# First down projection of a hybrid decoder layer with weights as the wide operand and results by rows

## The chip, the cores and the metric

The kernel runs on one core of one Trainium2 chip. The metric is the device time of one execution in microseconds (us), lower is better. The core's engines appear below as PE (TensorE, matrix products; PEld is its loading of the stationary operand), DVE (VectorE), ACT (ScalarE), POOL (GpSimd) and SP (SyncE, which here only issues DMAs). Each engine works through its own queue in order, and waits on semaphores for what other engines and transfers produce.

## The reference

One layer over 512 tokens of 1024 features in fp32: two feed-forward blocks around a mixer, each added to the running x.

```python
x = x + 0.5 * swiglu(rmsnorm(x, g1), w1_gate, w1_up, w1_down)
x = x + hybrid_mixer(rmsnorm(x, gm))        # projections, sparse attention, RG-LRU, gates, output
x = x + 0.5 * swiglu(rmsnorm(x, g2), w2_gate, w2_up, w2_down)
out = rmsnorm(x, gf)

def rmsnorm(x, g):
    return x * rsqrt(mean(x * x, axis=-1) + 1e-6) * g
def swiglu(x, w_gate, w_up, w_down):
    return (silu(x @ w_gate) * (x @ w_up)) @ w_down      # 1024 -> 2816 -> 1024
```

The change lies in the last product of the first block, `(...) @ w1_down`, a 512 x 2816 by 2816 x 1024 product, and in the norm that follows it, the one ahead of the mixer.

## The kernel before, in words

**Layout.** x is kept transposed: eight tiles `x[k]` of 128 features by 512 tokens, one `[P, 2*S]` buffer `xs` for two of them. A product of fp32 operands is made of fp32r products: each operand is split into a rounded high part and the rest (`wh`, `wl` of a weight tile, `ch`, `cl` of an activation tile, `yh`, `yl` of a normed x), and three products are summed: high by high, high by low, low by high. Splitting costs one ACT copy (high) and one DVE subtraction (low) for each tile.

**The first down projection** (`block_down`, lines 1060 to 1289, with `products1` and `results1`, 1504 to 1560). It is a block scheme of seven products p = 1, 2, 5, 6, 3, 7, 4 in that order, in place of eight; each p contracts 1408 of the 2816 features for 256 tokens and 512 output columns, in eleven steps of 128. The list `steps` holds 77 steps (p, j) and one empty place; two steps share one 128 x 1024 weight tile `wh`/`wl`, a "unit". p = 1, 2 and 4 take plain blocks of the weights (`wr`); the sums of weight blocks for p = 5, 6, 3 (`sm`) and p = 7 (`s`) are built by DMA: SP loads a base, and POOL issues DMAs that add another block onto it. The activation operands `ch`/`cl` (joined ones: `cx`) are made from `ha` and `hb`, the hidden activations.

In the version before, the weights are the stationary operand, 128 columns at a time (four groups m), and 256 tokens stream past. For most p a step is 12 matmuls of 256 columns. For p = 1 and 6 (`BROAD`) the high and low activation parts lie side by side in one 512-wide tile, so that a step is four matmuls of 512 and four of 256; the two halves of the result are added behind that. p = 6, 7 and 4 accumulate on in the banks of p = 1, and p = 3 in those of p = 5 (`CHAIN`). When a p is complete, DVE adds half of its result to the quarter of x that `ADDS` names (`x<-mm,x`): p = 1 and 2 to the first 256 tokens of features 0 to 511, p = 6 and 3 to the last 256 tokens of the same, p = 5 and 7 to the last 256 tokens of features 512 to 1023, p = 4 to the first 256 of these.

**The order around the turns.** The emission order is by hand (`with tc.manual_schedule`, lines 1584 to 1620), and each engine takes its instructions in that order. `d1.tasks_at(i)` emits what step i carries: fetches five to nine steps ahead, and four steps ahead of a unit its split. `late1` hangs further work on steps: the operands y of the mixer's norm (`norm_tile`, `norm_round`). Where p = 7 ends and p = 4 begins (`turn_`, steps 65 and 66) the next p overwrites the same banks, so the results must be out of them first; the products of the last two and of the next steps are there interleaved by groups of m. The last three steps (`TAIL`) are emitted group by group, so that the results of the first group leave while the second is multiplied.

**The norm ahead of the mixer.** Each finished part of x is squared on ACT (`sq`) and summed over features into `acc` by DVE; four matmuls with the matrix `mean` sum over partitions (`norm_steps`), then `sd` (ACT square root, with a load of its table), `rs` (DVE reciprocal), and four transposes that spread rs to `rstd`. The mixer's first product, `i0` (lines 1900 to 1925), starts at once with unnormalised operands y[k] = x[k] * gain, k = 0 to 7, three matmuls of 512 columns for each k; the scaling by `rstd` comes afterwards. Behind the y of the last tiles on ACT's queue stand the splits of the indexer's key weights (`wh<-wr 128x8x40` and `128x8x24`) and of the next mixer weights.

## Time and profile before

| what | us |
|---|---|
| median of 3 runs (1036.27 to 1037.15) | 1036.5 |
| the profiled execution, span from first to last instruction | 1034.5 |
| PE busy in the span | 1027.6 (99%) |
| DVE busy | 906.6 (88%) |
| ACT busy | 710.4 (69%) |
| POOL busy | 203.3 (20%) |
| mean DMA rate | 199 GB/s |

The profiled execution is known by its span alone; the runs' median is 2.0 us above it, what lies before the first and behind the last instruction in a timed run. A row of the timeline reads: start in us, duration in us, engine, line, operation, output<-inputs, shape, and how many in a row (x4). Matmuls are pipelined, so that their durations overlap; the distance between starts is what one costs. All engine operations of the kernel go through one recording helper and carry its line, L251; tiles tell them apart. The first down projection runs from 226.7 us to 336.7 us; the mixer and the second feed-forward block follow.

### The profile page before, as it was taken

Reading aid. Unit: us, or ns where it says so; the run is one execution under the profiler, and the core shown is the slowest. Engines: PE = TensorE matmul, PEld = TensorE weight load, DVE = VectorE, ACT = ScalarE, POOL = GpSimd, SP = SyncE. Lnnn points to the kernel's source line nnn. Section 1 sums busy time; section 2 is a strip of 40 time slices with the busy share of each in tenths; the row PEclk is TensorE's granted clock in tenths of the full one; section 3 lists DMA queues with packets and bytes.
Section 4 is the critical chain, followed back from the end, with each engine's and each line's share of the span. In section 5 each row is a group of like instructions: output and inputs, shape, how many; then the busy total and the mean of one; then the engine's idle time right before and its main releaser. Section 6 shows DMA issues by size and latency. Waiting matters only on the chain.

```text
span 1034.5 us, 16004 instructions
## 1 busy us (share of the span) xinstructions
PE 1027.6 (99%) x5600; PEld 892.9 (86%) x5600; DVE 906.6 (88%) x1571; ACT 710.4 (69%) x1195; POOL 203.3 (20%) x255
## 2 busy tenths in 40 slices
PE   9999999999999999999999999999999999999997
PEld 8898888899999888888888888888988888898886
DVE  7988999889998888998989966777889999989886
ACT  8856766666766669978896674367666766657864
POOL 1613333213240011111101110013432333110000
PEclk9999999999999999999999999999999999999999
DMA  9969999897994463343469987793889999987564
GB/s 355 201 171 216 222 238 216 192 275 194 183 244 152 149 181 101 107 128 107 122 187 282 278 212 209 208 295 62 193 226 245 215 221 227 205 203 225 167 189 164
DMA packets 92257, 206.01 MB, mean 199 GB/s; under 512 B 18576, under 2 KB 25872, under 8 KB 92176
## 3 DMA queue, kind: packets, MB, share of 16 engines
q1 hardware_dynamic: 59952, 141.75, 41.0%
q0 software_dynamic: 31936, 62.93, 35.0%
q8 instruction: 44, 0.72, 0.3%
q10 hardware_dynamic: 288, 0.31, 0.1%
q14 instruction: 37, 0.30, 0.1%
HBM read 185.02 MB, written 25.17 MB: 203 GB/s over the span
## 4 chain that ended last, share of the span: by engine, by line
PE 99%; DVE 0%; DVEq 0%; issue 0%
PE mm L251 72%; PE aux L251 27%; PE aux L1340 0%; DVE xr L251 0%; DVE o L251 0%; DVE sq L251 0%; DVEq L2568 0%; DVE rs L251 0%; DVE ss L251 0%
## 5 line engine op out<-in xcount | busy, mean ns | idle before, releaser
L251 DVE TENSOR_TENSOR wl<-wr,wh 128x1024 fp32r<-128x1024 f32 (+3 forms) x154 | 183.0, 1189 | 30.6 <-ACT wh L251 30.1
L251 ACT ACTIVATE wh<-wr 128x1024 fp32r<-128x1024 f32 (+2 forms) x155 | 158.8, 1026 | 43.4 <-PE mm L251 20.0
L251 PE MATMUL mm<-cm,wh 128*128 128x512 f32 (+1 forms) x736 | 167.0, 354 | 0.0
L251 PEld LDWEIGHTS mm<-cm,wh 128*128 128x128 f32 x736 | 126.3, 190 | 15.8
L251 PE MATMUL mm<-yn,wh 128*128 128x512 f32 x420 | 130.8, 393 | 0.0
L251 PE MATMUL aux<-cm,wh 128*128 128x512 f32 (+1 forms) x472 | 119.5, 383 | 0.0
L251 PE MATMUL mm<-cm,wl 128*128 128x256 f32 x608 | 108.3, 282 | 0.0
L251 PEld LDWEIGHTS aux<-cm,wh 128*128 128x128 f32 x472 | 86.0, 188 | 15.6
L251 PEld LDWEIGHTS mm<-cm,wl 128*128 128x128 f32 x608 | 92.2, 190 | 4.7
L251 PEld LDWEIGHTS mm<-yn,wh 128*128 128x128 f32 x420 | 77.0, 188 | 14.8
L251 PE MATMUL mm<-yn,wl 128*128 128x512 f32 x210 | 81.9, 390 | 0.0
L251 PE MATMUL aux<-cm,wl 128*128 128x256 f32 x456 | 70.5, 282 | 0.0
L251 ACT ACTIVATE wh<-a 128x1024 fp32r<-128x1024 f32 (+1 forms) x68 | 57.1, 842 | 18.2 <-DVE a L251 17.2
L251 DVE TENSOR_TENSOR wl<-a,wh 128x1024 fp32r<-128x1024 f32 (+1 forms) x68 | 64.7, 952 | 5.5 <-ACT wh L251 5.0
L251 PE MATMUL mm<-yh,wh 128*128 128x512 f32 (+1 forms) x168 | 65.4, 392 | 0.0
L251 PE MATMUL mm<-yl,wh 128*128 128x512 f32 (+1 forms) x168 | 65.3, 390 | 0.0
L251 PEld LDWEIGHTS aux<-cm,wl 128*128 128x128 f32 x456 | 63.1, 191 | 1.9
L251 PE MATMUL mm<-yh,wl 128*128 128x512 f32 x160 | 62.1, 390 | 0.0
L251 ACT ACTIVATE tu<-mm 128x512 f32<-128x512 f32 (+1 forms) x57 | 28.2, 495 | 43.8 <-PE mm L251 43.7
L251 DVE TENSOR_TENSOR wl<-s,wh 128x1024 fp32r<-128x1024 f32 (+1 forms) x46 | 49.3, 1080 | 1.2 <-ACT wh L251 1.1
L251 ACT ACTIVATE wh<-s 128x1024 fp32r<-128x1024 f32 (+1 forms) x46 | 43.0, 943 | 7.1 <-PE mm L251 2.0
L251 PEld LDWEIGHTS mm<-yn,wl 128*128 128x128 f32 x210 | 39.4, 188 | 8.5
(400 smaller groups left out, 2596.8 us busy)
## 6 DMA issues: line engine op xcount, KB each, us to landing
wr<-wm SPq DMA_DIRECT2D x39, 512.0 KB, 3.6
w<-w2d SPq DMA_DIRECT2D x20, 512.0 KB, 7.0
wr<-w SPq DMA_DIRECT2D x20, 512.0 KB, 3.5
wr<-w1u SPq DMA_DIRECT2D x19, 512.0 KB, 5.9
s<-w2u SPq DMA_DIRECT2D x36, 256.0 KB, 4.4
wr<-w2u SPq DMA_DIRECT2D x18, 512.0 KB, 5.6
s<-w2u POOLq DMA_DIRECT2D x36, 256.0 KB, 6.3
s<-w1u SPq DMA_DIRECT2D x32, 256.0 KB, 4.8
```

The costliest lines, as they stand in the source:

```text
L251: return call(*args, **kw)
```

## The change

The operands of the first down projection change places. The activations (128 tokens at a time, two groups m) are now the stationary operand and the weights stream past, 512 columns wide; the result of a p is two tiles of 128 tokens by 512 features, by rows instead of transposed. Every step of every p is six matmuls of 512 columns, and `BROAD` is gone with its additions.

The rows are added onto a second copy of the input: `xrow`, the untransposed x, is loaded by four DMAs of 512 KB into `xr` (two buffers that `QI` takes later). A quarter of x that is complete by rows is turned back into `x[k]`: after p = 2, p = 3 and p = 7 by two DMA transposes each (`spread_row`: ACT copies the fp32 rows into planes of 16-bit halves, `xp`; SP issues the transpose into `xq`; `merge_row`: two ACT copies put the halves together again in x), and after p = 4 by eight TensorE transposes into two `aux` banks (`turn_rows`, called inside the mixer's i0), from which ACT and DVE make the last y. The squares of the norm are summed along the rows by ACT itself (`square_row`, with accumulation into `ssr`), which takes the place of `acc` and of the `mean` matmuls.

```diff
-    def products1(i, ms=range(KD // 2)):
+    def products1(i, ms=range(2)):
...
-            T.matmul(o, h[:, c], th, start=starts, stop=False, **opens)
-            T.matmul(o, h[:, c], tl, start=False, stop=False, **opens)
-            T.matmul(o, l[:, c], th, start=False, stop=i == lasts1[p], **opens)
+            o, th, tl = chain1(p, m), sh[:, m * QB:(m + 1) * QB], sl[:, m * QB:(m + 1) * QB]
+            T.matmul(o, th, h, start=starts, stop=False, **opens)
+            T.matmul(o, tl, h, start=False, stop=False, **opens)
+            T.matmul(o, th, l, start=False, stop=i == lasts1[p], **opens)
...
+    def square_row(m, half):
+        A.activation(work("sq"), rows1(m, half), AF.Square, accum_out=ssr[:, half * NQ + m:half * NQ + m + 1])
+
+    def spread_row(m, half):
+        u, turned1[m, half] = work("xp"), awork("xq")
+        A.copy(bits(u).rearrange("p (k h t) -> p k h t", k=NQ, h=2), bits(rows1(m, half)).rearrange("p (k t h) -> p k h t", k=NQ, h=2))
+        nc.sync.dma_start_transpose(bits(turned1[m, half]).rearrange("p (g r) -> p g r", r=QB), bits(u))
+
+    def merge_row(m, half):
+        src = bits(turned1.pop((m, half))).rearrange("p (k h r) -> p k r h", k=NQ, h=2)
+        for i in range(2):
+            to = bits(xs[2 * half + i]).rearrange("p (k r h) -> p k r h", k=2, h=2)
+            A.copy(to[:, :, m * QB:(m + 1) * QB, :], src[:, 2 * i:2 * i + 2])
...
+    for i, (s_, half) in zip((1, 2, 8, 14), ((0, 0), (1, 1), (1, 0), (0, 1))):
+        then1(i, load_rows, s_, half)
+    for p, s_, half, at in ((2, 0, 0, (2, 4, 8)), (3, 1, 0, (2, 4, 8)), (7, 1, 1, (1, 3, 7))):
+        for m in range(2):
+            then1(lasts1[p] + at[0] + m, spread_row, 2 * s_ + m, half)
+            then1(lasts1[p] + at[1] + m, square_row, 2 * s_ + m, half)
+            then1(lasts1[p] + at[2] + m, merge_row, 2 * s_ + m, half)
...
-        for ms in ((0, 1), (2, 3)):
+        for m in range(2):
             for i in range(last, len(steps)):
-                products1(i, ms)
-        rounds = [norm_round(k, lo) for k in range(KD // 2, KD)]
-        for m in range(KD // 2):
+                products1(i, (m,))
             result1(4, m, *ADDS[4][0])
-            next(rounds[m])
-            if m:
-                next(rounds[m - 1], None)
-        next(rounds[-1], None)
+            square_row(m, 1)
...
+    def turn_rows(m):
+        if not ends:
+            ends.extend(aux() for _ in range(2))
+        for k in range(NQ):
+            T.transpose(ends[k // 2][:, (k % 2 * 2 + m) * QB:(k % 2 * 2 + m + 1) * QB], rows1(m, 1)[:, k * QB:(k + 1) * QB], ident)
+        if not m:
+            return
+        for k in range(NQ):
+            src, (h, l) = ends[k // 2][:, k % 2 * HS:(k % 2 + 1) * HS], y[NQ + k]
+            A.activation(h[:, lo], src, AF.Copy, scale=col(V_GM, NQ + k))
+            V.scalar_tensor_tensor(l[:, lo], src, col(V_GM, NQ + k), f(h[:, lo]), op0=ALU.mult, op1=ALU.subtract)
...
             for k in range(n):
+                if i == 0 and k in (0, 2):
+                    turn_rows(k // 2)
```

Three places of the order matter below. The first is SP's queue at the first steps of the projection; `sj`, `wr` and `sm` are weight tiles on their way in. Before:

```order
L239 DMA wr_2650<-w1d 128x1024
L239 DMA sj_2680<-w1d 128x512
L239 DMA wr_2682<-w1d 128x1024
L239 DMA sj_2712<-w1d 128x512
L239 DMA wr_2714<-w1d 128x1024
L239 DMA wr_2742<-w1d 128x1024
L239 DMA wr_2770<-w1d 128x1024
L239 DMA wr_2796<-w1d 128x1024
L239 DMA s_536_3348<-w1d 128x512
```

After, the same place (`wr_2635` is the earlier `wr_2650`, the weights of the last pair of p = 1; `wr_2665` is `wr_2682`, the first pair of p = 2):

```order
L238 DMA wr_2635<-w1d 128x1024
L238 DMA xr_2637<-xrow 128x2x512
L238 DMA xr_2638<-xrow 128x2x512
L238 DMA sj_2663<-w1d 128x512
L238 DMA wr_2665<-w1d 128x1024
L238 DMA sj_2689<-w1d 128x512
L238 DMA wr_2691<-w1d 128x1024
L238 DMA wr_2715<-w1d 128x1024
L238 DMA xr_2638<-xrow 128x2x512
L238 DMA wr_2740<-w1d 128x1024
L238 DMA wr_2762<-w1d 128x1024
L238 DMA xr_2637<-xrow 128x2x512
```

Four row loads of 512 KB stand among the weight loads, two of them ahead of the first pair of p = 2; the two transposes of the quarter that p = 2 completes come behind these rows and ahead of the first `s` load.

The second place is the turn from p = 7 to p = 4. ACT's queue before, from the split of the last single weight tile (`sj`) on:

```order
L251 ACTIVATE wh_3740<-sj_2712 128x512
L251 ACTIVATE sq_3758<-x_95 128x512
L251 ACTIVATE yh_3761<-x_95,vt 128x512
L251 ACTIVATE wh_3789<-wr_3687 128x1024
L251 ACTIVATE sq_3799<-x_95 128x512
L251 ACTIVATE yh_3802<-x_95,vt 128x512
```

ACT's queue after, from the same split on (`xq` holds the transposed rows of the quarter that p = 3 completed):

```order
L250 ACTIVATE wh_3427<-sj_2689 128x512
L250 COPY x_94<-xq_3359 128x2x256
L250 COPY x_95<-xq_3359 128x2x256
L250 COPY x_94<-xq_3370 128x2x256
L250 COPY x_95<-xq_3370 128x2x256
L250 ACTIVATE wh_3455<-wr_3397 128x1024
L250 ACTIVATE yh_3459<-x_94,vt 128x512
```

Four merging copies, which need both transposes, stand ahead of the split `wh_3455` of a pair of p = 4. DVE's queue at that turn before (`mm` are the banks of p = 7's result):

```order
L251 TENSOR_TENSOR wl_3741<-sj_2712,wh_3740 128x512
L251 TENSOR_TENSOR acc<-acc,sq_3758 128x512
L251 SCALAR_TENSOR_TENSOR yl_3762<-x_95,vt,yh_3761 128x512
L251 TENSOR_TENSOR wl_3790<-wr_3687,wh_3789 128x1024
L251 SCALAR_TENSOR_TENSOR x_96<-mm_2611,x_96 128x256
L251 SCALAR_TENSOR_TENSOR x_96<-mm_2614,x_96 128x256
```

DVE's queue there after:

```order
L250 TENSOR_TENSOR wl_3428<-sj_2689,wh_3427 128x512
L250 TENSOR_TENSOR wl_3456<-wr_3397,wh_3455 128x1024
L250 SCALAR_TENSOR_TENSOR yl_3460<-x_94,vt,yh_3459 128x512
L250 SCALAR_TENSOR_TENSOR xr_2638<-mm_2608,xr_2638 128x512
L250 SCALAR_TENSOR_TENSOR xr_2638<-mm_2612,xr_2638 128x512
```

Between the weight split `wl` and p = 7's first result a `yl` has moved in, and there are two results of 512 instead of four of 256.

The third place is ACT's queue where the projection ends and the mixer begins. Before:

```order
L251 ACTIVATE sq_4005<-x_97 128x256
L251 ACTIVATE yh_3886<-x_97,vt 128x256
L251 ACTIVATE sq_4011<-x_97 128x256
L251 ACTIVATE yh_3905<-x_97,vt 128x256
L251 ACTIVATE wh_4018<-wr_3866 128x8x40
L251 ACTIVATE wh_4018<-wr_3866 128x8x24
L251 ACTIVATE wh_4066<-wr_3910 128x1024
L251 ACT_TABLE_LOAD
L251 ACTIVATE sd_4086<-aux_4081,epst 128x4
```

After, the same place:

```order
L250 ACTIVATE sq_3597,ssr<-xr_2637 128x512
L250 ACTIVATE sq_3609,ssr<-xr_2637 128x512
L250 ACTIVATE wh_3611<-wr_3521 128x8x40
L250 ACTIVATE wh_3611<-wr_3521 128x8x24
L250 ACTIVATE wh_3665<-wr_3539 128x1024
L250 ACT_TABLE_LOAD
L250 ACTIVATE sd_3656<-sd_3656,epst 128x4
L250 ACTIVATE yh_3565<-aux_3647,vt 128x256
L250 ACTIVATE yh_3569<-aux_3647,vt 128x256
L250 ACTIVATE yh_3579<-aux_3648,vt 128x256
L250 ACTIVATE yh_3583<-aux_3648,vt 128x256
```

The four `yh` of the last tiles have moved from ahead of the key weights' splits to behind the square root.

More of the change, by code (lines that the diff above doesn't have):

```diff
@@ L51 @@
 SUMS_AT = -12, -11, -7, -5, -2
-BROAD = (1, 6)
 WIDE, FIRST_FOLD = (2, 5, 3), 3
@@ L256, in hybrid_kernel @@
 @with_exitstack
-def hybrid_kernel(ctx, tc, xt, vec, w1s, w1u, w1d, wm, wki, wrg, watt, wrnn, wout, w2u, w2d, gf, out):
+def hybrid_kernel(ctx, tc, xt, xrow, vec, w1s, w1u, w1d, wm, wki, wrg, watt, wrnn, wout, w2u, w2d, gf, out):
     nc = tc.nc
@@ L382, in waits, with norm_steps @@
         return which, tiles, aux, att, slots, key, mm, tmps, late, rounded
-    def norm_steps(*sums, blocks=range(NQ)):
-        pc, n = psaux(), len(blocks)
-        for i, a in enumerate(sums):
-            if i:
-                yield waits("PE", a)
-            for j, b in enumerate(blocks):
-                T.matmul(pc[:, j * QB:(j + 1) * QB], a[:, b * QB:(b + 1) * QB], mean, start=i + j == 0,
-                         stop=i == len(sums) - 1 and j == n - 1)
-        yield waits("ACT", pc)
-        sd = small.tile([P, NQ], F32, tag="st", name=nm("sd"))[:, :n]
-        A.activation(sd, pc.rearrange("p (b c) -> p b c", c=QB)[:, :n, 0], AF.Sqrt, bias=epst)
+    def norm_steps(*sums, blocks=range(NQ), total=None):
+        n = len(blocks)
+        sd = small.tile([P, NQ], F32, tag="st", name=nm("sd"))[:, :n]
+        if total is not None:
+            yield waits("DVE", total)
+            V.tensor_add(sd, total[:, :n], total[:, n:])
+            yield waits("ACT", sd)
+            A.activation(sd, sd, AF.Sqrt, scale=1.0 / D, bias=epst)
+        else:
+            pc = psaux()
+            for i, a in enumerate(sums):
+                if i:
+                    yield waits("PE", a)
+                for j, b in enumerate(blocks):
+                    T.matmul(pc[:, j * QB:(j + 1) * QB], a[:, b * QB:(b + 1) * QB], mean, start=i + j == 0,
+                             stop=i == len(sums) - 1 and j == n - 1)
+            yield waits("ACT", pc)
+            A.activation(sd, pc.rearrange("p (b c) -> p b c", c=QB)[:, :n, 0], AF.Sqrt, bias=epst)
         yield waits("DVE", sd)
@@ L1131, in block_down @@
                7: lambda n: ra[n], 4: lambda n: a(n, lo), 2: lambda n: b(n, lo)}
-        broad = lambda p: not made and p in BROAD
         def operand(p, n):
@@ L1291, in take @@
             return [parts_of(t) for t in tasks.pop(i, ())]
-        d.take, d.task, d.whole = take, task, {}
+        d.take, d.task = take, task
         d.ends = [{st[0]: i for i, st in way if st} for way in (list(enumerate(steps))[::-1], enumerate(steps))]
@@ L1490, in hybrid_kernel, with rows1, load_rows @@
     firsts1, lasts1 = d1.ends
[L1492 removed]
+    xr1, ssr, turned1 = [], const.tile([P, 2 * NQ], F32, name="ssr"), {}
+    U16 = mybir.dt.uint16
+    bits = lambda ap: ap.bitcast(U16)
+    def rows1(m, half):
+        return xr1[m // 2][:, m % 2, half * S:(half + 1) * S]
+    def load_rows(s_, half):
+        if not xr1:
+            for t in ("pth", "ptl"):
+                xr1.append(ptp.tile([P, NQ * S], F32, tag=t, name=nm("xr")).rearrange("p (m c) -> p m c", m=2))
+        c = slice(half * S, (half + 1) * S)
+        Q.dma_start(xr1[s_][:, :, c], xrow[s_ * HS:(s_ + 1) * HS, c].rearrange("(m p) c -> p m c", m=2))
     def chain1(p, m):
[L1495 to L1497 removed]
+        key = CHAIN.get(p, p), m
         if key not in banks1:
[L1499 to L1507 removed]
+            banks1[key] = psum("aux" if p == 2 else "mm")
+        return banks1[key]
+    def products1(i, ms=range(2)):
         if steps[i] is None:
@@ L1578, in hybrid_kernel @@
-    for k in range(KD // 2, KD):
-        then1(index[4, k - KD // 2], next, rounds[k], None)
-        then1(index[4, k - KD // 2 + 1], next, rounds[k], None)
+    for i, (s_, half) in zip((1, 2, 8, 14), ((0, 0), (1, 1), (1, 0), (0, 1))):
[5 more added lines that the diff above has]
+            then1(lasts1[p] + at[2] + m, merge_row, 2 * s_ + m, half)
@@ L1947, in hybrid_kernel @@
     QI = []
-    for k in ("pth", "ptl"):
-        q = ptp.tile([P, NQ * S], F32R, tag=k, name=nm("QI"))
-        QI.extend(q[:, j * S:(j + 1) * S] for j in range(4))
     KV, VV, QS = [], [], []
@@ L1998, in normalize @@
     def normalize():
-        yield waits("PE", acc, late=0.1)
-        yield from norm_steps(acc)
+        yield from norm_steps(total=ssr)
         ready.add("norm")
```

94 lines of the change are left out of this document (22 added, 72 removed).

## The prediction

> **What bounds the kernel now.** I read the page's totals first, then the chain of waits, then the busy time of each engine by stretches, then the timeline at the two ends of the stage that is changed.
>
> ```profile
> span 1034.5 us, 16004 instructions
> PE 1027.6 (99%) x5600; PEld 892.9 (86%) x5600; DVE 906.6 (88%) x1571; ACT 710.4 (69%) x1195; POOL 203.3 (20%) x255
> ...
> PE 99%; DVE 0%; DVEq 0%; issue 0%
> ```
>
> PE is busy for 99% of the span, and the chain that ends last lies 99% on it. So a microsecond of PE work that is removed is a microsecond of time, and every PE wait that is added is one too; work on other engines counts only where PE comes to wait for it. The stretches, one for the projection and two inside it:
>
> ```profile
> core 0: us, PE busy (x) PEld busy (x) DVE busy (x) ACT busy (x) POOL busy (x), PEclk, DMA share, GB/s
> 226.70:336.70 110.00, 110.00 (x838) 106.24 (x837) 101.31 (x179) 72.73 (x118) 25.98 (x31) 1.00 0.82 193
> ...
> 257.00:272.00 15.00, 15.00 (x127) 15.00 (x127) 15.00 (x25) 10.41 (x17) 3.50 (x4) 1.00 1.05 184
> 300.00:313.00 13.00, 13.00 (x110) 13.00 (x110) 12.70 (x24) 8.56 (x16) 4.96 (x8) 1.00 1.09 275
> ```
>
> PE has no gap in the projection, at the full clock (1.00), but DVE is at 92% and the DMA engines at 0.82, and around 257 to 272 and 300 to 313 the DMA share is above 1: they are full. The stage can shrink by PE's savings, but has little room for new transfers just there.
>
> **The change: matmuls.** What a matmul costs is the distance between starts. First 256 columns, then p = 1's mixed form, then 512 columns in the second down projection, whose steps already have the form that the change gives the first.
>
> ```profile
> 269.78 0.28 PE L251 MATMUL aux<-ch,wh 128*128 128x256 f32 x1
> ...
> 271.58 0.28 PE L251 MATMUL aux<-ch,wh 128*128 128x256 f32 x1
> ```
>
> ```profile
> 231.37 0.64 PE L251 MATMUL mm<-ch,wl 128*128 128x256 f32 x4
> ...
> 236.96 0.28 PE L251 MATMUL mm<-ch,wl 128*128 128x256 f32 x1
> ```
>
> ```profile
> 957.61 0.39 PE L251 MATMUL mm<-wh,cl 128*128 128x512 f32 x1
> ...
> 959.88 0.39 PE L251 MATMUL mm<-wl,ch 128*128 128x512 f32 x1
> ```
>
> Fifteen intervals in 1.80 us make 0.120 us for 256 columns; ten in 2.27 make 0.227 for 512. Of 77 steps 55 are twelve of the first (1.44 us), and 22 (p = 1 and 6) take 5.59/4 = 1.40. That is 79.2 + 30.8 = 110.0 us, the stretch above. After, all 77 are six of 512: 462 x 0.227 = 104.7 us. Gain: 5.3 us.
>
> [...]
>
> **Mean matmuls out, row transposes in.** Rows at the end of the projection carry this and the next part but one:
>
> ```profile
> 338.47 0.49 ACT L251 ACTIVATE yh<-x,vt 128x256 fp32r<-128x256 f32 x1
> ...
> 338.87 1.66 ACT L251 ACTIVATE wh<-wr 128x320 fp32r<-128x320 f32 x3
> 339.00 0.48 DVE L251 SCALAR_TENSOR_TENSOR yl<-x,vt,yh 128x256 fp32r<-128x256 f32 x1 [0.22 <-ACT yh L251]
> ...
> 340.16 1.05 PE L251 MATMUL aux<-mean,acc 128*128 128x128 f32 x8
> ...
> 340.55 1.28 ACT L251 ACT_TABLE_LOAD   x1
> ...
> 340.96 0.48 PE L251 MATMUL mm<-yh,wh 128*128 128x512 f32 x1
> 341.28 0.40 PE L251 MATMUL mm<-yl,wh 128*128 128x512 f32 x1
> ...
> 341.84 0.26 ACT L251 ACTIVATE sd<-aux,epst 128x4 f32<-128x4 f32 x1
> ```
>
> The eight go out: 0.80 us, and 0.09 because the next 512 takes 0.32 instead of 0.23. Eight transposes of 128 x 128 come in, in two groups, so the switch is paid twice: 0.8 + 0.18. Net +0.1.
>
> **Row loads.** 2 MB more on SP's queue, half of it ahead of the first pair of p = 2. Loads of 512 KB on that queue land in 5.0 us, and ACT already waited for them:
>
> ```profile
> ACT wh L251 <- DMA wr<-w1d: 4.4, 3, 2.1
> ```
>
> These waits cost PE nothing, because splits are made four steps ahead. Between 0 and 1.5 us (the longest wait less the part that lead takes); I take 0.2.
>
> **The transposes.** The operations that are new to ACT and DVE here have near rows in the second block, and so has the transpose:
>
> ```profile
> L251 DVE SCALAR_TENSOR_TENSOR xr<-mm,xr x12: 677/682/693, 940.6 to 1027.0; 128x512 f32<-128x512 f32 x12
> L251 ACT COPY xr<-x x8: 1342/1350/1360, 931.3 to 999.2; 128x1024 uint16<-128x1024 uint16 x8
> L251 ACT ACTIVATE sq<-xr x7: 612/613/634, 957.0 to 1026.3; 128x512 f32<-128x512 f32 x7
> L251 ACT ACTIVATION_READ_ACCUMULATOR sq<-xr x7: 185/186/187, 957.5 to 1026.8; 128x1 f32 x7
> ```
>
> ```profile
> L251 ACT COPY xp<-x x6: 1029/1030/1031, 668.3 to 696.6; 128x1024 uint16<-128x1024 uint16 x6
> ```
>
> The next two are lists of DMAs: around the second block's transposes (890 to 912 us), and in the first projection where p = 2's would be issued (254 to 273). The last is that list for the whole projection; its last number is the median from issue to landing.
>
> ```profile
> DMA packets 9489, 4.55 MB, mean 207 GB/s; under 512 B 8560, under 2 KB 8560, under 8 KB 9487
> ...
> q0 software_dynamic: 535, 0.96, 29.7%
> ...
> x<-planes SPq DMA_TRANSPOSE x8, 4.8
> ```
>
> ```profile
> q0 software_dynamic: 1186, 3.06, 94.7%
> ```
>
> ```profile
> sm<-w1d POOLq DMA_DIRECT2D x15, 512.0 KB, 6.7
> wr<-w1d SPq DMA_DIRECT2D x13, 512.0 KB, 5.0
> ...
> s<-w1d SPq DMA_DIRECT2D x10, 256.0 KB, 7.8
> s<-w1d POOLq DMA_DIRECT2D x10, 256.0 KB, 10.7
> ```
>
> For a pair of rows ACT has 2 spreads (1.03), 2 squares (about 0.7 with the accumulator read, which overlaps) and 4 merges of half the size of the 1.35 copy (0.68): 6.2 us. After p = 2 they fall into about eight steps, 10.9 us; ACT's idle share between 257 and 272 is 4.59/15, so 3.3 us are free. ACT falls behind by 2.9 at most, and its lead of four steps covers that, unless it also stands waiting for a landing. Queued behind a merge on ACT are the splits `wh`, for which DVE and then PE wait. A transpose waits on SP's queue for its spread, and behind it stand the `s` loads of p = 7, fetched ten and more steps ahead: a wait of one copy there costs nothing.
>
> So the landing time L of a transpose decides. It was 4.8 us in the second block, where POOL's queue (q0) took 30% of the engines' time. Here that queue takes 95% where p = 2's transposes are issued, and p = 3's meet p = 7's adds; SP's own loads beside such adds took 7.8 us as a median, POOL's 10.7. L lies between 4.8 and about 12; I take 9.6, nearer to the rows beside the adds. ACT comes to the first merge some 10.8 us after the issue (eight steps of 1.36), to the merges after p = 3 some 8.9 us after theirs (merges at six steps, behind three splits). So p = 2's pair costs 0 by landing; I take 0.4 for ACT's lag (0 to 2.9).
>
> [...]
>
> **The turn from p = 7 to p = 4.** The next p overwrites the banks, so the result stands between:
>
> ```profile
> 317.06 0.74 DVE L251 SCALAR_TENSOR_TENSOR yl<-x,vt,yh 128x512 fp32r<-128x512 f32 x1
> ...
> 318.02 1.06 ACT L251 ACTIVATE wh<-wr 128x1024 fp32r<-128x1024 f32 x1 [1.06 <-PE mm L251]
> ...
> 319.11 1.23 DVE L251 TENSOR_TENSOR wl<-wr,wh 128x1024 fp32r<-128x1024 f32 x1 [1.30 <-ACT wh L251]
> ...
> 320.25 1.41 DVE L251 SCALAR_TENSOR_TENSOR x<-mm,x 128x256 f32<-128x256 f32 x4
> ...
> 320.82 0.47 PE L251 MATMUL mm<-cx,wh 128*128 128x256 f32 x2
> ```
>
> ACT's split starts when PE frees its buffer, 24 matmuls (2.88 us) ahead of 320.82, at S = 317.94. The split of DVE starts at S + 1.17, the results at S + 2.31, and p = 4 starts just in time. After, PE wants to go on at S + 2.72, but DVE has `wl` to S + 2.31, a `yl` of about 0.7 to S + 3.0, and a result of 0.68 to S + 3.7. Firm stall: 1.0 us. Ahead of that split on ACT now stand the four merges, 2.4 to 2.7 us in place of a square and a `yh` with 1.06 us of idle behind them (2.3 in all, 2.2 at the new pace): 0.3 more. And each microsecond of L above 8.9 adds one: 0.7 at 9.6. Turn: 2.0 us, from 1.0 to 4.4 (L = 12).
>
> **The end of the stage.** Let T be the end of p = 4's last product. Before, the last `yh` were made first, and PE never waited. After, ACT does: result at T + 0.9, the last square to T + 1.65, then the three weight splits, the table load and `sd`, which took from 338.87 to about 342.05, 3.2 us: the first of the four `yh` starts at T + 4.8, is written at T + 5.2, its `yl` at T + 5.7. PE reaches that operand (k = 4) after four groups of transposes and products: 2 x 0.5 + 4 x 0.68 = T + 3.7. It waits 1.5 and, for the `yl`, about 0.2 more: 1.7 us (1.2 if the squares overlap better; 2.4 if the weights' splits wait too). What comes after, `sd` and `rstd`, stands no later than before against PE.
>
> **Hidden edits.** DVE loses the `acc` additions and half of its result overhead, ACT the copies of p = 6: at nothing, as neither bounds PE. The p = 7 transposes are issued when POOL's adds are over, since the last of them built p = 7's weights: L near 4.8, no cost, as six steps (8.2 us) lie ahead of the merge; about 1.4 us if L were 9.6.
>
> **The sum.** -5.3 + 0.1 + 0.2 + 0.4 + 2.0 + 1.7 = -0.9 us. The profile's span of 1034.5 would become 1033.6; the runs' median lies 2.0 above the span (1036.5), so 1035.6 us. 0.2%, about 2.1 us, is what a measurement can tell from no change: within 1034.4 and 1038.6 is "same".
>
> **Rivals.**
> Landing in time (faster): L at or below 8.9 and little lag give -5.3 + 0.1 + 1.2 (turn) + 1.5 (end) = -2.5, 1034.0; with an end stall near zero, 1032.5. For it speak the 4.8 us of the second block and the 7.8 of SP's loads, against it the DMA share above 1.
>
> Transposes starve (slower): they sit on SP's queue beside POOL's adds, in small pieces (8560 packets for eight, 67 for each of 16 engines). The sum is -1.6 at L = 8.9, and each further microsecond adds one at the turn, from 10.8 on another at p = 2; from L = 11.7 it is above +2.1, and at 12.5 it is +3.7: 1040.2. For it speak the share of 1.05 with POOL's adds back to back, and the 10.7 us of POOL's queue; against it, that SP's loads there landed in 7.8. [...]
>
> The gain isn't there: if 512 columns with the operands changed over cost as much as two of 256 (0.240), the stage's products take 462 x 0.240 = 110.9 us, 6.2 more than in the sum, which becomes +5.3: 1041.8. Against it stands that 0.227 is measured on just this form. I give it 2 in 100, within the slower ones. [...]
>
> DMA becomes the bound: the stretch's 0.82 x 110 = 90 us for 193 GB/s x 110 us = 21 MB mean 4.3 us a MB, so that 2 MB add 9, against 104.8 us in all. It fits on the whole, but not around 257 to 272; it would show as late `sm`, some 1 to 3 us more than the forecast, 1037 to 1039.
>
> **How the numbers follow.** Forecast and its neighbours within 0.2%: 0.43. In time: 0.32 faster. Starving, DMA-bound or no gain: 0.25 slower. The range takes the firm part of the faster case and the beginning of the starving one, 1033.0 to 1039.5.
>
> **What would show it.** In the changed profile: matmuls of 512 at 0.227, the stage near 104.8 us plus PE gaps; a gap of 1 to 4 us ahead of p = 4, with DVE `xr<-mm,xr` as releaser; one of 1.7 us in i0 ahead of the fifth operand, released by ACT `yh`; transposes at 8 to 11 us after p = 2 and p = 3, and near 5 after p = 7. It is wrong if there is no gap at the end of the stage, if ACT waits long for `xq`, or if gaps stand in places that are not named.

## The result, and the profile after

| | median, us | lowest to highest |
|---|---|---|
| before, 4 runs | 1036.4 | 1036.3 to 1037.2 |
| after, 4 runs | 1045.75 | 1041.7 to 1047.3 |

The ratio is 1.0082, with a 95% interval from 1.0062 to 1.0103: slower by 9 us, where the prediction had 1035.6 and a range up to 1039.5. The runs before lie within 1 us, those after within 6: something in the new version is decided anew in each execution. The profiled execution is the slowest of the four (1047.3; span 1045.5, 11.0 us above the span before), so the waits read from it below are those of the longest of the four.

The totals and the chain of the page after:

```profile
span 1045.5 us, 15221 instructions
PE 1029.7 (98%) x5226; PEld 874.8 (84%) x5226; DVE 898.5 (86%) x1529; ACT 721.6 (69%) x1205; POOL 203.9 (20%) x255
...
PE 89%; DMA 5%; DVE 2%; ACT 2%; issue 1%; DVEq 0%; ACTq 0%; POOLq 0%
PE mm L250 67%; PE aux L250 22%; DMA xq<-xp 2%; DMA wr<-w1d 1%; DMA s<-w1d 1%; DVE wl L250 1%; ACT wh L250 1%; DMA ha<-cr 1%; DVE xr L250 1%; PE aux L1332 0%; DVE sj L250 0%; ACT x L250 0%; DVE cl L250 0%; ACT ch L250 0%; DVE o L250 0%
```

The chain is no longer PE alone: a tenth of it now lies on transfers and on the engines that wait for them, and the first of these is the transpose, `xq<-xp`. By stretches:

```profile
core 0: us, PE busy (x) PEld busy (x) DVE busy (x) ACT busy (x) POOL busy (x), PEclk, DMA share, GB/s
226.70:250.00 23.30, 21.69 (x95) 17.03 (x95) 17.61 (x25) 11.39 (x16) 1.97 (x2) 1.00 0.82 263
250.00:270.00 20.00, 19.60 (x85) 15.41 (x84) 17.67 (x24) 16.43 (x26) 8.28 (x9) 1.00 0.98 185
270.00:290.00 20.00, 18.11 (x77) 13.68 (x76) 17.22 (x29) 15.73 (x27) 4.59 (x6) 1.00 1.04 207
290.00:310.00 20.00, 20.00 (x89) 16.36 (x88) 19.03 (x37) 11.53 (x18) 9.46 (x13) 1.00 1.05 231
310.00:330.00 20.00, 16.29 (x68) 13.12 (x67) 13.83 (x22) 16.27 (x27) 2.73 (x5) 0.93 0.85 186
330.00:350.00 20.00, 18.56 (x84) 14.77 (x83) 10.23 (x15) 15.08 (x29) 0.00 (x0) 0.98 0.57 163
```

Only the stretch from 290 to 310 is as the prediction wanted the whole stage: PE busy all the time, with a matmul every 0.23 us. In two stretches PEclk is below 1.00, which no stretch of the projection was before. The two long waits are seen in the timeline of PE. The turn from p = 7 to p = 4:

```profile
323.45 0.39 PE L250 MATMUL mm<-wl,ch 128*128 128x512 f32 x1
327.55 1.19 PE L250 MATMUL mm<-wh,cx 128*128 128x512 f32 x2 [3.71 <-DVE xr L250]
328.54 0.63 PE L250 MATMUL mm<-wl,cx 128*128 128x512 f32 x1
...
330.24 0.83 PE L250 MATMUL mm<-wh,cx 128*128 128x512 f32 x2
330.91 0.40 PE L250 MATMUL mm<-wl,cx 128*128 128x512 f32 x1
```

And in the mixer's first product, ahead of the fifth operand:

```profile
347.48 0.40 PE L250 MATMUL mm<-yh,wl 128*128 128x512 f32 x1
349.30 0.50 PE L250 MATMUL mm<-yh,wh 128*128 128x512 f32 x1 [1.43 <-ACT yh L250]
...
352.06 0.63 PE L250 MATMUL mm<-yl,wh 128*128 128x512 f32 x1
352.48 0.63 PE L250 MATMUL mm<-yh,wl 128*128 128x512 f32 x1
```

After both waits matmuls start 0.427 us apart (352.06 to 352.48) instead of 0.227: half the clock (0.50), for 3.4 us each time. Taking 0.227 off the distance between the starts of successive matmuls and adding up what is left gives what the waits cost by place, here for the changed kernel and for the versions tried below (the last column is the time from the mixer's first product to the second down projection, 586.6 us before). Each row is one execution: the slowest of four for the changed kernel, the fastest of four for rows_late and merges_late, so differences of 1 or 2 us between rows can be chance.

| stops, us | 226 to 255 | 255 to 275 | 275 to 310 | turn, last results, first product of the mixer | mixer to second down |
|---|---|---|---|---|---|
| after | 2.6 | 0.9 | 3.1 | 5.4 + 4.0 | 590.1 |
| rows_late | 0 | 2.3 | 1.8 | 2.8 + 2.6 | 588.8 |
| merges_late | 0.3 | 1.4 | 1.2 | 0.8 + 4.3 | 588.4 |
| end_held | 1.3 | 1.2 | 2.1 | 4.1 + 2.0 | 587.9 |
| all_held | 0 | 1.3 | 1.3 | 1.1 + 2.9 | 588.0 |
| best2 | 0 | 1.9 | 1.3 | 0.4 + 2.0 | 586.4 |
| no_rows | 0 | 0 | 0 | 2.1 | 586.4 |

For the changed kernel that is 16.0 us; with the 5.3 saved and 0.1 for transposes the span should be 10.8 us longer, and it is 11.0. The longest of the waits themselves, PE's first and then ACT's, from 226 to 360 us:

```profile
PE mm L250 <- DVE xr L250: 3.7, 1, 3.7
PE mm L250 <- DVE wl L250: 1.8, 4, 0.5
PE mm L250 <- ACT yh L250: 1.4, 1, 1.4
PE aux L250 <- DVE wl L250: 1.0, 2, 0.5
```

```profile
ACT wh L250 <- DMA wr<-w1d: 11.0, 5, 5.2
ACT wh L250 <- PE mm L250: 5.2, 6, 1.5
ACT x L250 <- DMA xq<-xp: 3.8, 2, 2.0
```

ACT's wait for weights has grown from 4.4 to 11.0 us, and the merging copies (`x`) stand 3.8 us for transposes. My theory at this point: the stops have four causes of their own (row loads ahead of weights; merges on ACT ahead of splits; the order of ACT at the end; a half clock behind long stops), each of which can be undone alone. The rival: 2 MB of rows and 1.5 MB of transposes are too much for DMA engines that were full already (a share of 1.10 from 290 to 310 us before), and a cause mended at one place comes back at another.

### The profile page after: what moved, and what is told of

The parts are those of the page before. It is cut to its first block, busy times and chain, and to the rows that moved or that the text cites. A ratio compares the mean times of both kernels' runs of the same rounds, so it can differ in the third digit from the quotient of the medians.

```text
span 1045.5 us, 15221 instructions
## 1 busy us (share of the span) xinstructions
PE 1029.7 (98%) x5226; PEld 874.8 (84%) x5226; DVE 898.5 (86%) x1529; ACT 721.6 (69%) x1205; POOL 203.9 (20%) x255
## 4 chain that ended last, share of the span: by engine, by line
PE 89%; DMA 5%; DVE 2%; ACT 2%; issue 1%; DVEq 0%; ACTq 0%; POOLq 0%
PE mm L250 67%; PE aux L250 22%; DMA xq<-xp 2%; DMA wr<-w1d 1%; DMA s<-w1d 1%; DVE wl L250 1%; ACT wh L250 1%; DMA ha<-cr 1%; DVE xr L250 1%; PE aux L1332 0%; DVE sj L250 0%; ACT x L250 0%; DVE cl L250 0%; ACT ch L250 0%; DVE o L250 0%
## 5 line engine op out<-in xcount | busy, mean ns | idle before, releaser
L250 PE MATMUL mm<-wl,ch 128*128 128x512 f32 (+1 forms) x240 | 93.9, 391 | 1.8 <-DVE wl L250 1.8
L250 PE MATMUL mm<-wh,ch 128*128 128x512 f32 (+1 forms) x240 | 93.3, 389 | 0.5 <-ACT wh L250 0.5
L250 PE MATMUL mm<-wh,cl 128*128 128x512 f32 (+1 forms) x240 | 93.3, 389 | 0.0
L250 ACT ACTIVATE wh<-a 128x1024 fp32r<-128x1024 f32 (+1 forms) x68 | 57.1, 842 | 18.2 <-DVE a L250 17.2
```

The source lines that it names most:

```text
L250: return call(*args, **kw)
```

## The experiments

**Undoing one cause each.** The first four versions ran on one chip, the later ones on others, each beside the kernel before.

```diff
-    for i, (s_, half) in zip((1, 2, 8, 14), ((0, 0), (1, 1), (1, 0), (0, 1))):
+    for i, (s_, half) in zip((4, 15, 17, 58), ((0, 0), (1, 1), (1, 0), (0, 1))):     # rows_late
```

> The changed kernel with the four row loads put later (after steps 4, 15, 17 and 58 instead of 1, 2, 8 and 14), nothing else. Theory (the stalls add up by place, each with its own cause): PE's gaps between 243 and 252 us, 2.6 us in the changed kernel's profile, go, and perhaps the 0.9 us at 265 to 269, where DVE was behind; some 3 us less than the changed kernel, about 1042.5. Rival (the 2 MB are too much for full DMA engines, wherever they go): the gaps only move to later steps, and the time stays within 1 us of 1045.7.

Measured: 1042.3 us (1040.2 to 1045.4), 1.0056 of before (1.0037 to 1.0076). The stops before 255 us are gone, as the theory had it; but 2.3 us stand between 255 and 275, where there were 0.9. A part has moved. That the loads' place makes the stops before 255 doesn't rest on this profile alone: the six versions profiled with the rows in the changed kernel's places have 0.3 to 2.6 us there, the nine that load them later have none.

```diff
-    ... ((2, 0, 0, (2, 4, 8)), (3, 1, 0, (2, 4, 8)), (7, 1, 1, (1, 3, 7))):
+    ... ((2, 0, 0, (2, 4, 20)), (3, 1, 0, (2, 4, 13)), (7, 1, 1, (1, 3, 7))):       # merges_late
-        then1(lasts1[3] + 10 + k, lambda k=k: y.append(norm_tile(k, V_GM, False)))
+        then1(lasts1[3] + 15 + k, lambda k=k: y.append(norm_tile(k, V_GM, False)))
```

> The changed kernel with the merging copies after p = 2 put twelve steps later and those after p = 3 five steps later, behind the turn, with the operands made from them. Theory (ACT stands waiting for transposes, with weight splits queued behind): the 3.1 us of gaps at 279 to 291 go, and of the 5.4 us at the turn all but 0.3 to 1; some 7 us less than the changed kernel, about 1038.5. Rival (ACT has too much to do, not too long to wait): the copies cost the same elsewhere, gaps of 3 us or more stay after 280 or appear after the turn, and the time is above 1042.

Measured: 1041.05 us (1039.4 to 1042.4), 1.0046 (1.0029 to 1.0063). The turn falls from 5.4 to 0.8 us and the stops after 275 from 3.1 to 1.2: there ACT did wait with splits queued behind. But a new stop of 2.0 us stands ahead of the last results, since ACT now has merges, spreads, squares and operands on its hands in twelve steps: both views had a part.

```diff
             square_row(m, 1)
-        mixer_begin()
-        mixer_prepare()
...
                 if i == 0 and k in (0, 2):
                     turn_rows(k // 2)
+                    if k:
+                        ready.add("turned")     # the norm waits for it
+                        mixer_begin()
+                        mixer_prepare()
```

> The changed kernel with the last four yh, made from the turned rows, ahead of the splits of the key weights, of the next weights, the table load and the square root on ACT. Theory: the gap of 1.6 us ahead of the fifth operand of the mixer's first product goes, and with it the eight or nine matmuls at half clock behind it; 3 to 4 us less than the changed kernel, about 1042. Rival (the wait only moves to the scaling, since rstd comes later): a gap as long appears in the next products of the mixer, and the time stays within 1 us of 1045.7.

> The three edits together. Theory: the stage keeps the 5.3 us that the wide matmuls save, less about 1 us at the turn and at the start of the mixer and 0.1 for transposes: 1032 to 1034, faster than before. Rival (DMA engines full in the first half of the stage): late weights still stop PE by 2 to 5 us, and the time is 1035 to 1038.

Measured: 1062.85 us (1059.7 to 1063.8) and 1059.3 us (1057.7 to 1060.5), 17 and 14 us above the changed kernel. Neither view had that. The mixer's order is laid out by a planner from its own estimates, and this edit changed what it saw: from the 31st matmul of the mixer on the traces have the products in another order, and the time from the mixer's first product to the second down projection became 610 and 608 us, from 590. So these two say nothing on the end of the stage. They were done again with the planner seeing the calls in the old order, while ACT's and DVE's instructions of the key weights and of the norm are issued behind the last operands:

```diff
             self.plan.add(self.which, self.cost(name, aps, given, "accum_out" in kw), outs, aps[1:])
+            if self.plan.held is not None and self.which in ("ACT", "DVE"):
+                self.plan.held.append((call, args, kw))      # issued behind the last yh and yl
+                return
             return call(*args, **kw)
```

> The changed kernel with the last four yh and yl ahead of the key weights' splits, the table load and the square root, as in the earlier attempt, but with everything behind the start of the mixer in the order of the changed kernel (the planner of the mixer's order sees no difference). Theory: the gap of 1.6 us ahead of the fifth operand goes, and with it the matmuls at half clock behind it (some 2 us): 3 to 4 us less than the changed kernel; the 17 us that the earlier attempt lost were the planner's other order of the mixer. Rival (rstd comes later, and that costs what the operand gains): within 1 us of the changed kernel, with a gap in the mixer's second or third product.

Measured: 1041.9 us (1041.2 to 1043.9), 1.0056 (1.0041 to 1.0071): 3.8 us less than the changed kernel. The mixer's products have the changed kernel's order again. The wait for the fifth operand and the half clock behind it are gone, 4.0 us, and the rival has its part too: a stop of 1.7 us ahead of the transposes of `rs`, which now come later. So the edit itself is worth 2.0 us (4.0 less 2.0 in the table); the rest of the difference lies in stops that it doesn't touch, before 255 us and at the turn. In all_held the three go together, with the merges after p = 3 only three steps late, inside the turn, where ACT was idle (and the norm's first step two later):

```diff
-    ... ((2, 0, 0, (2, 4, 8)), (3, 1, 0, (2, 4, 8)), (7, 1, 1, (1, 3, 7))):
+    ... ((2, 0, 0, (2, 4, 20)), (3, 1, 0, (2, 4, 11)), (7, 1, 1, (1, 3, 7))):       # all_held
```

> The changed kernel with row loads late, merges after p = 2 late and after p = 3 inside the turn (three steps later than in the change), and the last operands first with the mixer's order kept. Theory: what remains of the stalls is about 3 us between 255 and 290, where DVE is busy without a break, under 1 us at the turn and under 2 us at the last results: 1034 to 1036, at or below the kernel before. Rival (ACT is overfull behind the turn): a gap of 2 us or more at the last results, and 1037 to 1039.

Measured: 1038.0 us (1037.6 to 1038.4; 11 runs), 1.0015 (1.0006 to 1.0024). The time is the rival's, but not its cause, a gap of 2 us at the last results: 2.6 us of stops stay from 255 to 310, 1.1 at and behind the turn, 1.0 at the last results, 1.9 ahead of `rs`.

**The half clock by itself.** To the kernel before, which has none of the changed kernel's transfers, DVE subtractions that nobody needs were added ahead of p = 7's results, two and seven of them:

```diff
             if i == turn_:
+                for _ in range(2):      # gap_1us; 7 in gap_4us
+                    V.tensor_sub(work("sq"), x[0], x[1])
                 results1(i)
```

> The kernel before with two extra DVE subtractions of 128x512 (1.2 us) ahead of p = 7's results, so that p = 4 starts some 1.2 us late and nothing else changes. Theory (a stop of PE costs its length, and a long one a stretch at half clock behind it): a stop this short costs its length alone, 1.2 to 1.5 us, with the granted clock at 1.0 behind it. Rival (every stop of PE has the slow clock behind it, whatever its length): 3 us or more.

> The kernel before with seven such subtractions (4.2 us) ahead of p = 7's results. Theory: 4.2 us of stop, and behind it matmuls at half clock for 2 to 4 us, which cost 1 to 2 us more: 5.5 to 6.5 us above the kernel before. Rival (the slow matmuls of the changed kernel come from its DMA traffic or its transposes, not from the stop): 4.2 to 4.5 us, all matmuls at full clock.

Measured: 1038.0 and 1043.6 us, 1.5 and 7.1 above before, in one run each. The stretches of the two kernels around the stop (PE's busy time, the clock, the DMA share and rate), the shorter first:

```profile
320.90:322.30 1.40, 0.36 (x4) 1.00 0.44 64
322.30:326.00 3.70, 3.70 (x31) 1.00 0.31 122
```

```profile
321.40:325.70 4.30, 0.29 (x3) 0.86 0.39 122
325.70:331.20 5.50, 5.46 (x25) 0.50 0.19 54
```

A stop of 1.2 us costs 1.2 and keeps the clock; one of 4.2 us is followed by 5.5 us at half clock, in which 25 matmuls take what 46 would: 4.2 + 2.5 of the 7.1. So a stop alone can make the slow matmuls. Between the two its length doesn't decide. The stop of 1.8 us (from start to start) ahead of the fifth operand cost the clock in the changed kernel, and in rows_late, at the same place and of the same length (341.64 to 343.46), it did not; nor did rows_late's stop of 2.9 us at the turn. The traces' record of the granted clock shows what differed. Between its changes lie 94, 1, 6, 1 and 202 times 3.413 us in the changed kernel's trace, and 301 times that in the trace of before: windows of 3.41 us, whose place differs from one execution to the next (borders at 327.25 us in the changed kernel and at 322.10 in rows_late). A stretch at half clock is one such window each time in the changed kernel and two, 6.8 us, in gap_4us. The windows around the stops, in the changed kernel and then in rows_late:

```profile
323.84:327.25 3.41, 0.00 (x0) 1.00 0.03 11
327.25:330.67 3.42, 3.12 (x8) 0.50 0.72 201
330.67:334.08 3.41, 3.41 (x16) 1.00 0.99 210
347.73:351.15 3.42, 1.95 (x6) 1.00 0.41 143
351.15:354.56 3.41, 3.41 (x9) 0.50 0.03 8
```

```profile
318.68:322.10 3.42, 1.97 (x9) 1.00 0.42 164
322.10:325.51 3.41, 2.33 (x10) 1.00 0.55 162
342.57:345.98 3.41, 2.47 (x8) 1.00 0.27 108
```

A full window is counted with 16 of these matmuls. Behind the two with none and with 6 the next window has half the clock; behind those of rows_late, with 8, 9 and 10, it has not. Of two windows with 7, the one in plain_copy was followed by the half clock and the one in rows_26_35 was not. In rows_late a border between two windows cuts either stop, at 322.10 and at 342.57. So two stops of the same length cost that length in rows_late and some 1.5 us more in the changed kernel, and what was seen to differ is where the windows' borders lay.

The other way to try it was to fill the two stops of the changed kernel with matmuls into a free bank:

```diff
+            if i == turn_:      # fill: 3.2 us; 6 more ahead of the fifth operand
+                spare = psum("aux")
+                hw = d1.units[(i - 1) // 2][0][:, :S]
+                for n in range(14):
+                    T.matmul(spare, d1.turned[steps[i]][0][:, :QB], hw, start=n == 0, stop=n == 14 - 1)
```

> The changed kernel with work for TensorE that nobody uses: 14 matmuls of 512 columns (3.2 us) into a free bank between p = 7 and p = 4, and 6 (1.4 us) ahead of the fifth operand of the mixer's first product. Theory (a long stop costs its length and then a stretch at half clock): p = 4 and the fifth operand start when they did, since DVE and ACT set that, but the clock stays at 1.0; 3 to 4 us less than the changed kernel, about 1042. Rival (the half clock has another cause, such as the load or the transposes): the slow matmuls stay and the time is the changed kernel's or more.

Measured: 1052.1 us (1050.5 to 1052.9). As a time it is of no use, as the planner again laid the mixer out in another order (597 us instead of 590). In the stage it does what the theory says. The stretches behind the turn and behind the filled wait run at full clock:

```profile
325.00:328.00 3.00, 2.84 (x13) 1.00 0.54 175
328.00:331.00 3.00, 3.00 (x15) 1.00 0.68 117
347.00:350.00 3.00, 2.97 (x12) 1.00 0.05 19
```

**Is it the transpose, or its place?**

```diff
-        nc.sync.dma_start_transpose(bits(turned1[m, half]).rearrange("p (g r) -> p g r", r=QB), bits(u))
+        nc.sync.dma_start(bits(turned1[m, half]), bits(u))       # plain_copy
```

> The changed kernel with each of the six DMA transposes replaced by a plain DMA of the same 256 KB between the same tiles (the rows are not turned, so this computes something else). Theory A (a transpose is slow of itself: small packets, a long time on SP's queue): the copies land in 4 to 5.5 us where the transposes took 6.5 to 10, and the stops after p = 2 and at the turn shrink by 2 us or more. Theory B (what is slow is the place, beside POOL's adds): the copies land in 6 to 9 us after p = 2 and p = 3, and the stops shrink by less than 1 us.

Measured: 1041.4 us in one run. The copies landed in 5.1 and 6.8 us after p = 2 and in 5.6 and 5.3 after p = 3, the transposes of the changed kernel in 7.8 and 10.0, and 7.3 and 6.5. The stop at the turn fell to 1.3 us and those after 275 to 1.3, 5.8 us less in all, of which 1.5 is the half clock behind the turn. That is theory A in the stops, though one landing (6.8) is where theory B had it. All six copies landed sooner than the transposes in their places, these four by 1 to 3 us; there is one profile of each version.

**What is left from 255 to 290.** best puts the end of the stage right (key weights' splits where ACT waits anyway, square root behind the last operands, the next weights behind it) and moves DVE's four `sj` sums five steps ahead:

```diff
-            for at, o, m, n in ((20, "w5", 2, 3), (21, 2, 2, 0), (22, 0, 0, "w5"), (23, 1, 1, 0)):
+            for at, o, m, n in ((15, "w5", 2, 3), (16, 2, 2, 0), (17, 0, 0, "w5"), (18, 1, 1, 0)):    # best; not in best2
...
+        for call, args, kw in plan.later:       # behind rs: the next weights' split, the copies of the last rows
+            call(*args, **kw)
```

> The version with late row loads, late merges and the last operands first, with four more moves: row loads after steps 4, 12, 14 and 58; DVE's four sums of single weight blocks (sj) five steps earlier, where DVE waits, out of the stretch from 256 us in which it is busy without a break; the squares of p = 7's rows behind the last yh of the upper halves; the key weights' splits ahead of the last yh again (ACT waits there for TensorE's transposes) and the next mixer weights' split, with the copies of the last rows, behind the square root. Theory: of the stops that are left, 2.4 us at 256 to 288 fall by half (DVE's backlog), 1.0 us at the last results and 1.9 us ahead of the transposes of rs nearly go: 1034 to 1035.5, faster than both kernels. Rival (DVE has more to do between 256 and 290 than the faster steps leave, wherever the sums stand; 2 us of stops remain there): 1036 to 1037, no faster than before.

Measured: 1039.0 us, above both views, and from 1035.3 to 1042.75 in 12 runs, 1.0023 (1.0010 to 1.0035). The end is as wanted: from the mixer's first product on 586.5 us, as before. The stops from 275 to 310 are 5.6 us in the profiled run. Its DMAs between 244 and 300 us (the last number is the median from issue to landing):

```profile
sm<-w1d POOLq DMA_DIRECT2D x10, 512.0 KB, 14.0
ha<-cr POOLq DMA_DIRECT2D x5, 256.0 KB, 8.4
xr<-xrow SPq DMA_DIRECT2D x2, 512.0 KB, 10.0
xq<-xp SPq DMA_TRANSPOSE x2, 14.3
```

One of the two transposes took 19.4 us, and the additions onto `sm` behind it 12 to 17 us: a jam of the DMA engines, which moved 65 to 123 GB/s from 275 to 283 us at a share of 0.9 or more (185 on average from 244 to 300). From best2, which is best with sums and rows where all_held has them, one thing was then taken away at a time: DVE's sums, three of the row loads, the two transposes after p = 2. These three versions leave out what the result needs.

> The version before the last with its end (key weights' splits, last yh, square root, next weights in that order) and the row loads and sums where all_held had them (rows after steps 4, 15, 17 and 58, sums at steps 20 to 23). Theory: the first half is that of all_held, with 2.4 us of stops from 256 to 288, the end costs 1.5 us less than there: 1036 to 1037, level with the kernel before. Rival (the length of the DMA backlog is chance, not the place of the row loads): a spread of 5 us or more between runs, as in the version with the sums early.

> The same with DVE's four sums of single weight blocks left out (the products of the joined step then use wrong weights). If DVE's work is what stops PE between 256 and 290, 2.7 us of it less remove 1.5 to 2.4 us of stops: 1034 to 1035. If late transfers are, the stops stay: 1036 to 1037.

> The same with three of the four row loads left out (POOL writes zeros into these parts early, so that the results lack x there). If the row loads' transfers delay those behind them (ha<-cr, sm), the stops from 256 to 270 go, 1 us or more: 1035 or less. If DVE's work or the transposes are the cause, the time changes by less than 0.5 us.

> The same without the two DMA transposes after p = 2 (the merging copies read the planes as they are, so that quarter isn't turned). If the transposes among POOL's adds delay the sums of weights (sm), the stops from 278 to 290 go, 1 to 1.4 us: 1035 to 1035.5. If DVE's work is the cause, the time changes by less than 0.5 us.

```diff
+                parts_.setdefault(o, parts_[m])                              # no_sums, for the tensor_add
...
+        if (s_, half) == (0, 0):                                             # no_rows
+            Q.dma_start(xr1[s_][:, :, c], xrow[s_ * HS:(s_ + 1) * HS, c].rearrange("(m p) c -> p m c", m=2))
+        else:
+            nc.gpsimd.memset(xr1[s_][:, :, c], 0.0)
...
+        if (m, half) in ((0, 0), (1, 0)):                                    # no_turn2
+            turned1[m, half] = u
+            return
```

| | median, us | ratio to before |
|---|---|---|
| best2 | 1036.9 (1033.9 to 1037.6) | 1.0002 (0.9993 to 1.0010) |
| no_sums | 1039.1 (1035.6 to 1041.5) | 1.0021 (1.0011 to 1.0031) |
| no_rows | 1033.55 (1033.2 to 1034.0) | 0.9971 (0.9959 to 0.9982) |
| no_turn2 | 1036.55 (1036.1 to 1037.7) | 1.0000 (0.9991 to 1.0009) |

Without three row loads the whole stage runs as the prediction's first term has it, 104.8 us with 463 matmuls (a stop of 1.4 us at the last results stands behind it):

```profile
226.70:331.50 104.80, 104.64 (x463) 86.27 (x462) 91.77 (x137) 79.13 (x119) 29.28 (x34) 1.00 0.95 218
```

DVE's work alone isn't what stops PE between 255 and 290: no_rows has all of it and no stop there. It has a part: without the sums the stops before 275 fell from 1.9 to 0.3 us, but another jam came, with a transpose of 20.6 us and 5.5 us of stops. Both versions that take the sums out of this place, best and no_sums, run from 1035 to 1043 us; all_held, best2 and no_turn2, which leave them there, from 1034 to 1038. Whether a DVE that is earlier there sets the jam off was not tried by itself. Without p = 2's transposes the time is the same within 0.4 us. The row loads are what stops PE there. How, the landings of DMAs from 244 to 300 us show, in best2 and then in no_rows:

```profile
sm<-w1d POOLq DMA_DIRECT2D x10, 512.0 KB, 7.8
ha<-cr POOLq DMA_DIRECT2D x5, 256.0 KB, 7.8
xr<-xrow SPq DMA_DIRECT2D x2, 512.0 KB, 7.2
xq<-xp SPq DMA_TRANSPOSE x2, 9.3
```

```profile
sm<-w1d POOLq DMA_DIRECT2D x10, 512.0 KB, 7.1
ha<-cr POOLq DMA_DIRECT2D x5, 256.0 KB, 3.8
xq<-xp SPq DMA_TRANSPOSE x2, 6.9
```

At 246 us two row loads run beside the additions onto `ha`, whose landing goes from 3.8 to 7.8 us; ACT's `ch` waits for these, and with it the splits behind, DVE's and PE. In best2 ACT stood 3.5 us for them, in no_rows not at all:

```profile
254.22 0.63 ACT L254 ACTIVATE ch<-ha 128x512 fp32r<-128x512 f32 x1 [3.54 <-DMA ha<-cr]
```

The last two versions put these loads behind the additions, on SP's queue after the two transposes, and the third of them further back:

```diff
-    for i, (s_, half) in zip((4, 15, 17, 58), ...
+    for i, (s_, half) in zip((4, 26, 35, 58), ...       # rows_26_35; 26 and 43 in rows_26_42
```

> best2 with the second and third row loads on SP's queue behind the two transposes after p = 2 (which pace them to about 266 us, when the additions onto ha are over), nothing else moved. If the row loads' delay of those additions (ha<-cr) is what stops PE between 256 and 290, the stops go and the time is 1034 to 1035, faster than both kernels. Rival (any place in the first half of the stage delays something that is needed soon, here the sums sm): stops of 2 us or more from 270 to 290, 1036 to 1038.

> The same with the third row load further back, behind the first two s loads (about 278 us; it is needed at about 288). By the first view as the other or a little less, 1033.5 to 1035; by the rival a stop at p = 6's results when the rows land late, 1036 to 1038.

Measured: 1036.7 us (1035.5 to 1038.8), 1.0007 (0.9998 to 1.0016), and 1035.4 us (1032.5 to 1043.1), 0.9992 (0.9976 to 1.0008). The stops from 255 to 275 are gone in both, which bears out how the rows did harm there, and one of 2.3 us or 1.2 us stands at 279. It isn't late `sm`, which the rival had, though these landed in up to 11.3 us: DVE stands at p = 5's results for the rows themselves, and a sum for ACT's `ch` and a split stand behind. The second row load, issued at 265.35 and 264.35, landed 13.2 and 12.9 us later:

```profile
278.68 1.29 DVE L254 SCALAR_TENSOR_TENSOR xr<-mm,xr 128x512 f32<-128x512 f32 x2 [3.60 <-DMA xr<-xrow]
```

```profile
277.36 1.29 DVE L254 SCALAR_TENSOR_TENSOR xr<-mm,xr 128x512 f32<-128x512 f32 x2 [2.42 <-DMA xr<-xrow]
```

So the places tried for this load were too early for `ha<-cr` or too late for p = 5. That no place is free, as the rival says in general, isn't shown: none between steps 15 and 26 was tried, and two of rows_26_42's 11 executions took 1032.5 and 1032.6 us, while one took 1043.1. No version here beats the kernel before beyond the measurement; best2 is level with it, and no_rows, which is 3.0 us faster, leaves loads out.

## Why the prediction was wrong, point by point

- **Matmuls, -5.3:** right. One starts every 0.227 us, and the whole stage takes 104.8 us in no_rows. (462 x 0.227 is 104.9, so the gain by the prediction's own figures is 5.1.)
- **Mean matmuls and row transposes, +0.1:** right; four transposes take 0.4 us in the changed kernel's profile.
- **Row loads, +0.2 (0 to 1.5):** wrong, and the largest error that has one cause. The step was "These waits cost PE nothing, because splits are made four steps ahead". That held for waits of 2.1 us; with row loads ahead of them, three loads of `wr` landed in 8.5 to 9.5 us, ACT waited 5.2 in one piece, and 2.6 us came through to PE (0.3 to 1.4 in the five other profiles with the rows in these places). Put elsewhere, the same loads delayed `ha<-cr` or came late themselves: 1036.94 - 1033.55 = 3.4 us for three of them in best2's places. I had their volume as a rival ("DMA becomes the bound"), worked out that it "fits on the whole", and priced it at 1 to 3 us for `sm` alone. That rival was the nearest to what happened.
- **Transposes after p = 2, +0.4 (0 to 2.9):** 3.1. The landings, 7.8 and 10.0 us, were about those predicted (L = 9.6). The wrong step was where ACT stands then: "ACT comes to the first merge some 10.8 us after the issue". It came after 8.2 (264.84 to 273.04), just behind the landing, and to the second transpose's merges 8.3 us after its issue, 1.7 us ahead of its landing, since the spreads themselves had been late by then, waiting for DVE's results. Of the 3.1, 1.9 went with the merges (merges_late), and the other 1.2 went with the row loads (no_rows).
- **Turn, +2.0 (1.0 to 4.4):** 3.9 (2.5 to 3.0 in three other profiles with the merges in this place), the mechanism as described: DVE's `wl`, a `yl`, the results, with ACT standing at the merges for 2.05 us. The landing was short (7.3 and 6.5 us), and again the spread was late, so ACT reached the merge about 5.3 us after the issue instead of 8.9. That 3.9 lies within the range is partly luck: the landing was shorter than the 9.6 assumed, and ACT's lead was shorter by more.
- **End, +1.7:** the wait was 1.6.
- **What a stop costs:** left out. Every term counted a stop with its own length. Behind the turn a half clock added 1.5 us. Behind the wait at the end it added some 1.4 (4.0 us in all against 2.6 at the same place in rows_late, which kept the clock), and 0.8 more came from short waits for the operands behind the fifth.

The sum of the misses is 2.4 + 0.9 (275 and before, DVE behind after late weights) + 2.7 + 1.9 + 1.5 + 2.2 = 11.6, against 11.9 between the forecast of the span (-0.9) and what came (+11.0). No single term carries the miss, and these are the sizes in the slowest of the four executions. The rival of starving transposes had the sign but not the mechanism: L never reached its 11.7 in the changed kernel. It did in best and no_sums, as one jam in which the landings behind it grew to 12 to 17 us; what sets one off in some runs and not in others stays open. So does which of the changed kernel's stops make its runs differ by 6 us, as only one of them was profiled; where the clock's windows fall is one thing that differs, worth some 1.5 us for each of the two long stops.

## What to carry to other kernels

A saving on a bound engine is worth its size only if the transfers that pay for it have room: look at the DMA share of the very stretch (here up to 1.10 before, in a stage with 0.82), and price 2 MB there by what is queued beside it and how soon that is needed, not by the average over the stage (here 1.5 MB cost 3.4 us). A wait on an engine that works ahead is hidden only up to its lead, and the lead is what earlier waits have left of it: here ACT's waits of up to 2.1 us for weights cost PE nothing, and one of 5.2 us cost it 2.6. And look at the granted clock behind a stop of TensorE: here a stop of 1.8 us that left a 3.41 us window with 6 matmuls of 16 was followed by a window at half clock, some 1.5 us more, another of 1.8 us was not, nor was one of 1.2 us.

## What the runs showed of the hardware that was not expected

- The granted clock changed only at whole multiples of 3.41 us from its last change (94, 1, 6, 1 and 202 in the changed kernel's trace, 301 in the trace of before), and fell to 0.50 for whole windows of that length. In the projection and the mixer's first product it fell behind windows with none, 6 or 7 matmuls of 512 columns where a full one is counted with 16 (after, end_held, plain_copy), and not behind another with 7 (rows_26_35) or those with 8 and more; windows that also hold transposes are left out of this count. So a stop of 1.8 us had the half clock behind it where one window held it (after, plain_copy), and one of 2.9 us had not where a border cut it (rows_late).
- A DMA transpose of 256 KB held SP's queue for 1.2 us after p = 7, when POOL's adds were over, and for up to 4.0 us beside other traffic. In the changed kernel it landed in 3.1 and 4.8 us there and in 6.5 to 10 beside POOL's adds; in the two jams one took 19.4 and 20.6.
- A plain load of 512 KB issued between the transposes and POOL's adds took 13.2 and 17.2 us to land (rows_26_35); the changed kernel's four row loads took 5.6 to 9.4.
